# A two-layer encoder on one core: which gate products run in the seven-product scheme, and the order of the branches around the attention

## The chip, the cores and the metric

The kernel runs on one core of one Trainium2 chip. The metric is the device time of one launch in microseconds (us). TensorE (PE) multiplies matrices, VectorE (DVE) and ScalarE (ACT) work element by element, GpSimd (POOL) does little here, and SyncE (SP) issues the DMAs.

## The reference, cut to what matters

```python
for l in range(DEPTH):                              # DEPTH = 2, SEQ = D_MODEL = 1024
    h = rmsnorm(x, norm_pre[l])
    (hq, hf_f, hf_b, hi, hz, ca, cb, cz, sb, sc, sv, sz,
     aq, ak, av, az, mq, mz) = split_cols(h @ w_in[l])            # 256 columns each, ak and av 128
    y_hg = hgrn2_branch(hq, hf_f, hf_b, hi, hz, lower_bounds[l], hg_onorm[l])   # two-way scan
    y_cf = conformer_branch(ca, cb, cz, conf_dw_w[l], ...)        # 31-tap convolution, layer norm
    y_sc = short_conv_branch(sb, sc, sv, sz, sc_w[l])             # 3-tap convolution
    y_at = window_attention(aq, ak, av, ...) * jax.nn.silu(az)    # banded, blocks of 128
    mem_kv = rmsnorm(mem, mem_norm[l]) @ w_mem_kv[l]
    y_mem = memory_cross_attention(mq, mem_kv) * jax.nn.silu(mz)
    merged = None
    for n, yb in enumerate((y_hg, y_cf, y_sc, y_at, y_mem)):      # five branches
        term = jax.nn.sigmoid(h @ w_gate[l, n]) * (yb @ w_branch[l, n])
        merged = term if merged is None else merged + term
    x = x + rmsnorm(merged @ w_out[l], norm_post[l])
```

The gate `h @ w_gate[l, n]` is a product of 1024 by 1024 by 1024 for each of five branches, in float32.

## The kernel before

**Precision.** Each float32 operand is split into two parts, hi and lo (`split`: an ACT cast, then a DVE subtraction), and a product is three matmuls of 512 columns: hi by hi, lo by hi, hi by lo (`mm3`). A projection item (128 output columns, both token halves) is 48 such matmuls, and so is each of the two items of a branch output (`branch_items`).

**Order.** All engines' orders are written out by the program. `drive` takes items (`Item`: a preparation that loads and splits weights, and a body with the matmuls) from the generator `program` one after another. The next item's preparation is put out ahead of the present item's body. Between groups of three matmuls `plan.poll` puts out pieces of side work (scan, attention, convolution, norms) whose inputs should be ready by the planner's own clock. Side work with `idle="DVE"` is put out only when the planner's DVE clock is not ahead of its PE clock. An item with a `need` waits (`plan.wait`) until side work has set that flag; what this side work puts on PE stands ahead of the item's matmuls in PE's queue.

**Gates.** The five gates are 20 pairs of 128 output columns (branch n, pair g). A plain pair is two `gate_item`s of 48 matmuls. A pair in `strassen_items` uses seven products of half size, 7 x 12 = 84 matmuls; for it DVE forms sums of weights (`split_product`) and of results (`after`), and sums of the input h (`gate_forms`, put out once per layer). The second product waits for the flag `forms`. In the kernel before 15 pairs per layer go this way. The other five (branch 2, the short convolution, and pair 0 of branch 0) are plain: `sc_g` are eight plain items, `hg_g` two. Sums for pairs 1 to 3 are stored to DRAM (`mgd`) and loaded again in `after`.

**Order of a layer before.** Scan projections with the short convolution's projections between them (`hg`, `sc`), window attention projections (ak, av, aq, az for two halves g = 0, 1), the last short-convolution projection, the convolution branch's projections (cb, ca), hz, memory attention projections (mq, mz), branch output of the short convolution (`sc_b`), one plain gate, branch output of the scan, two plain gates, branch output of the window attention, five plain gates, two plain gates of the scan branch, cz (which needs the flag `cf`), branch outputs of memory and convolution, the seven-product stage, the output projection.

**Side work that matters here.** `workers` of the window attention run half g = 0 (flags `at{l}00`, `at{l}01`), then g = 1, eight blocks each; those of the memory attention run sixteen blocks. `conv` in `conformer_items` is the 31-tap convolution on DVE: per layer 60 multiply-adds over 1024 tokens, then a layer norm whose sums over channels are matmuls (`cf_mu`, `cf_var`). It begins at the flag `merge{l}`, which the first `sc_b` item sets, and ends with the flag `cf{l}`.

**Slots.** Most tensors lie in one pool of 38 slots of 128 x 1024 float32 (`slot`).

Names of tiles are those of the profile: `ps_g` plain gates, `ps_gX`, `ps_gY`, `ps_gZ` products, `ps_b` branch outputs, `ps_o` output projection, `at_*` and `m_*` window and memory attention, `cf_*` convolution branch, `h_*` scan. Nearly every row has line 112, the line of the helper `Meter` that passes each operation on.

Of the kernel before, what the change touches and what calls it, by code (L numbers as in the profile page):

```python
# [26 lines left out]
KC = D // P  # L27
# [179 lines left out]
def encoder(ctx: ExitStack, tc: tile.TileContext, a: dict, out: bass.AP):  # L207
# [398 lines left out]
    def conformer_items(l, hT, cs):  # L606
# [9 lines left out]
        us = [None, None]  # L616

        def conv():
            yield f"merge{l}"
            for j in range(2):  # L620
                yield f"cf_u{l}{j}"
                u = us[j]
                c = cs[j] = slot(f"cf_c{j}")
                mid = CONFK // 2
                dve.tensor_scalar(out=c, in0=u, scalar1=wt[:, j, mid:mid + 1], scalar2=vec[:, j, 0:1],
                                  op0=ALU.mult, op1=ALU.add)
                for k in range(CONFK):
                    if k == mid:
                        continue
                    o = k - mid  # L630
                    dst = c[:, max(0, -o):T - max(0, o)]
                    src = u[:, max(0, o):T - max(0, -o)]
                    dve.scalar_tensor_tensor(out=dst, in0=src, scalar=wt[:, j, k:k + 1], in1=dst,
                                             op0=ALU.mult, op1=ALU.add)
                    if k % 2:
                        yield
            for s in range(2):
                both = h2("cf_sum")
                dve.tensor_tensor(out=both, in0=cs[0][:, hs(s)], in1=cs[1][:, hs(s)], op=ALU.add)
                mu = yield from summed("cf_mu", mean_w, both)  # L640
                sq = []
                for j in range(2):
                    c = cs[j][:, hs(s)]
                    dve.tensor_tensor(out=c, in0=c, in1=mu, op=ALU.subtract)
                    sq.append(h2(f"cf_sq{j}"))
                    act.activation(out=sq[j], in_=c, func=AF.Square)
                dve.tensor_tensor(out=sq[0], in0=sq[0], in1=sq[1], op=ALU.add)
                var = yield from summed("cf_var", mean_w, sq[0])
                rs = h2("cf_rs")
                dve.tensor_scalar(out=rs, in0=var, scalar1=EPS, scalar2=None, op0=ALU.add)  # L650
                act.activation(out=rs, in_=rs, func=AF.Sqrt)
                dve.reciprocal(out=rs, in_=rs)
                yield
                for j in range(2):
                    c = cs[j][:, hs(s)]
                    dve.tensor_tensor(out=c, in0=c, in1=rs, op=ALU.mult)
                    th = h2("cf_t")
                    act.activation(out=th, in_=c, func=AF.Tanh, scale=half[:, j, 0:1], bias=half[:, j, 1:2])
                    dve.tensor_scalar(out=c, in0=c, scalar1=vec[:, j, 1:2], scalar2=vec[:, j, 2:3],
                                      op0=ALU.mult, op1=ALU.add)  # L660
                    dve.scalar_tensor_tensor(out=c, in0=th, scalar=1.0, in1=c, op0=ALU.add, op1=ALU.mult)
                yield
            plan.flags.add(f"cf{l}")
# [428 lines left out]
    def branch_items(l, n, ys, pbd, need=None, flag=None):  # L1092
# [4 lines left out]
        for q in range(2):  # L1097
            def prep(q=q):
                done = split_w(lambda raw: [(raw, wb[:, :, hs(q)])], [P, 2, HALF], f"b{n}{q}")

                def put():
                    if q == 0:
                        plan.wait(need)
                        for j, y in enumerate(ys):
                            yT.append((slot(f"yh{n}{j}", F32R), slot(f"yl{n}{j}", F32R)))
                            split(*yT[j], y)
                    return done()

                return put

# [101 lines left out]
    def strassen_items(l, groups, forms, pbd, mg, mgd, mT):  # L1212
# [4 lines left out]
        N = len(order)  # L1217
        raws, sums, banks, ws, late, pbs = {}, {}, {}, {}, [], {}
        state = {"loaded": 0, "split": 0}

        def load_group(gi):
            n, g = groups[gi]
# [33 lines left out]
        def merge(gi, dd, s, th):  # L1256
            n, g = groups[gi]
            m, pb = mg[g][s][:, dd, :], pbs[gi][dd]
            dve.scalar_tensor_tensor(out=th, in0=th, scalar=1.0, in1=pb[:, hs(s)], op0=ALU.add, op1=ALU.mult)
            dve.tensor_tensor(out=m, in0=m, in1=th, op=ALU.add)  # L1260

        def gate(gi, dd, s, th, src=None):
            act.activation(out=th, in_=th if src is None else src, func=AF.Tanh, scale=0.5)
# [13 lines left out]
        def after(k):  # L1277
# [3 lines left out]
            if name == "P1":  # L1281
# [3 lines left out]
                if g not in mg:  # L1285
                    mg[g] = []
                    for s in range(2):
                        mg[g].append(slot(f"mg{s}").rearrange("p (k t) -> p k t", k=2))
                        load(out=mg[g][s], in_=mgd[g][s])
                pbs.pop(gi - 1, None)  # L1290
                pbs[gi] = []
                for dd in range(2):
# [134 lines left out]
    with tc.manual_schedule(engines={mybir.EngineType.PE, mybir.EngineType.DVE, mybir.EngineType.Activation,  # L1427
# [30 lines left out]
        def program():  # L1458
# [22 lines left out]
            for l in range(NL):  # L1481
                o_hg, y_sc, y_cf, y_at, y_mem = ([None, None] for _ in range(5))
                lead, hg, hz = hgrn_items(l, hT, o_hg)
                if l == 0:
                    yield lead[0]
                    load_x(4, 5)
                    yield lead[1]
                    load_x(6, 7)
                    yield from lead[2:6] + mem_items[:2] + lead[6:7] + mem_items[2:] + lead[7:]
                else:  # L1490
                    yield from [mem_items[0], lead[0], mem_items[1], lead[1], mem_items[2], lead[2], mem_items[3]] + lead[3:]
                sc = short_conv_items(l, hT, y_sc)
                yield from hg[:1] + sc[0] + hg[1:] + sc[1][:3]
                yield from window_items(l, hT, y_at)
                yield from sc[1][3:]
                cf, cz = conformer_items(l, hT, y_cf)
                yield from cf
                mem = memory_attention_items(l, hT, kv, y_mem)
                yield from hz + mem
                mT = [[[None] * 4 for _ in range(2)] for _ in range(2)]  # L1500
                pbd = [[dram.tile([P, T], F32, name=f"pb{l}{n}{d}") for d in range(KC)] for n in range(5)]
                mgd = [[dram.tile([P, 2, HALF], F32, name=f"mg{l}{g}{s}") for s in range(2)] for g in range(4)]
                mg = {0: [None, None]}
                sc_g = [gate_item(l, 2, d, hT, pbd[2], mg[0], mgd[d // 2] if d > 1 else None, True)
                        for d in range(KC)]
                hg_g = [gate_item(l, 0, d, hT, pbd[0], mg[0], None, False) for d in range(2)]
                forms = {}
                plan.side(gate_forms(l, hT, forms))
                at_b = branch_items(l, 3, y_at, pbd[3], need=f"at{l}")
                mem_b = branch_items(l, 4, y_mem, pbd[4], need=f"mem{l}")  # L1510
                cz[1].flag = f"plain{l}"
                sc_b = branch_items(l, 2, y_sc, pbd[2])
                sc_b[0].flag = f"merge{l}"
                yield from sc_b
                yield from sc_g[:1] + branch_items(l, 0, o_hg, pbd[0]) + sc_g[1:3] + at_b + sc_g[3:] + hg_g
                yield from cz + mem_b + branch_items(l, 1, y_cf, pbd[1])
                groups = [(n, g) for g in range(4) for n in ((3, 4, 1) if g == 0 else (0, 3, 4, 1))]
                yield from strassen_items(l, groups, forms, pbd, mg, mgd, mT)
                gpost = cache(lambda l=l: row_bcast(a["norm_post"][l], f"gpost{l}"))
                x_src, hT = (x_mid if l else x_in), [None, None]  # L1520
# [43 lines left out]
```

## Time and profile before

| | us |
|---|---|
| median of 3 runs | 2317.66 (2316.72 to 2319.61) |
| the profiled execution | 2313.68 |
| its span, first to last instruction | 2311.9 |
| PE, DVE, ACT busy in the span | 2252.7, 1601.1, 971.9 |
| mean granted TensorE clock | 0.994 of full |

Busy time counts an instruction from its start to its end. Matmuls overlap in the pipeline, so a row of one shows about 0.39 us where the next begins 0.227 us later. "Idle before" is the time an engine stood still ahead of an instruction, with the instruction that ended it. Layer 1 runs from 0 to about 1172 us, layer 2 from there; the two look alike apart from their openings.

### The profile page before, as it was taken

What the parts mean: (1) busy time and instruction counts of PE and PEld (TensorE: products, weight loads), DVE (VectorE), ACT (ScalarE), POOL (GpSimd) and SP (SyncE); (2) the same over time, 40 slices, a digit from 0 to 9 for tenths busy, and PEclk for the clock granted to TensorE, in tenths of its full rate; (3) what the DMA queues carried; (4) which work ended last, traced back from release to release, by engine and by line L of the source; (5) the groups of instructions that cost most, each with busy time, mean ns of one, the idle gap of its engine ahead of it and who ended that gap; (6) DMA issues with size and microseconds to landing.
All of it is one profiled execution on the core that took longest, in us unless ns stands there. A gap on an engine that the chain in (4) does not pass through costs nothing.

```text
span 2311.9 us, 30491 instructions
## 1 busy us (share of the span) xinstructions
PE 2252.7 (97%) x11560; PEld 1843.1 (80%) x11560; DVE 1601.1 (69%) x2798; ACT 971.9 (42%) x1948; POOL 26.8 (1%) x41
## 2 busy tenths in 40 slices
PE   8899999999999999999999999999999999999998
PEld 6777788888887888887887778888878878888876
DVE  5767745446987688888667686453579787888865
ACT  5333335345434533335542433443453354333342
POOL 0000000000000000000110000000000000000000
PEclk9999999999999999999999999999999999999999
DMA  6102021103542633335440111211145525333344
GB/s 201 47 16 74 19 57 40 37 28 118 171 158 86 241 128 128 110 110 186 169 129 19 37 37 35 38 45 45 37 160 173 159 87 205 128 128 110 92 155 164
DMA packets 248019, 237.35 MB, mean 103 GB/s; under 512 B 29984, under 2 KB 191008, under 8 KB 247872
## 3 DMA queue, kind: packets, MB, share of 16 engines
q1 hardware_dynamic: 247872, 235.40, 31.4%
q8 instruction: 91, 1.49, 0.3%
q14 instruction: 56, 0.46, 0.1%
HBM read 177.69 MB, written 57.67 MB: 102 GB/s over the span
## 4 chain that ended last, share of the span: by engine, by line
PE 89%; DVE 7%; ACT 2%; issue 1%; DMA 0%; SPq 0%; POOL 0%; DVEq 0%; ACTq 0%; POOLq 0%
PE ps_gY L112 10%; PE ps_b L112 10%; PE ps_g L112 9%; PE ps_gX L112 7%; PE ps_o L112 7%; PE ps_gZ L112 7%; PE ps_hf L112 4%; PE h_s L112 3%; PE ps_hi L112 2%; PE ps_cb L112 2%; PE ps_hq L112 2%; PE ps_ca L112 2%; PE ps_sc L112 2%; PE ps_at_z L112 2%; PE ps_sz L112 2%; PE ps_hz L112 2%
## 5 line engine op out<-in xcount | busy, mean ns | idle before, releaser
L112 DVE TENSOR_TENSOR lo<-raw_g,hi 128x512 fp32r<-128x512 f32 x220 | 149.6, 687 | 95.0 <-ACT hi L112 94.7
L112 DVE SCALAR_TENSOR_TENSOR cf_c<-cf_u,cfw,cf_c 128x1009 f32<-128x1009 f32 (+14 forms) x120 | 153.0, 1275 | 3.0
L112 ACT CAST hi<-raw_g 128x512 fp32r<-128x512 f32 x220 | 133.6, 617 | 51.2 <-PE ps_gY L112 46.2
L112 PE MATMUL ps_b<-yh,lo 128*128 128x512 f32 x320 | 126.2, 394 | 7.5 <-DVE lo L112 7.5
L112 PE MATMUL ps_b<-yh,hi 128*128 128x512 f32 x320 | 128.8, 402 | 0.0
L112 PE MATMUL ps_b<-yl,hi 128*128 128x512 f32 x320 | 126.0, 394 | 0.0
L112 ACT COPY pb_out<-ps_b 128x512 f32<-128x512 f32 x160 | 91.1, 593 | 74.1 <-PE ps_b L112 57.2
L112 DVE TENSOR_TENSOR lo<-raw_in,hi 128x512 fp32r<-128x512 f32 x120 | 77.3, 686 | 46.2 <-ACT hi L112 46.0
L112 ACT ACTIVATE g_e<-g_e 128x512 f32<-128x512 f32 x60 | 38.0, 634 | 134.7 <-DVE g_e L112 134.7
L112 PE MATMUL ps_gX<-h_0h,hi 128*128 128x512 f32 x240 | 93.4, 389 | 0.0
L112 PE MATMUL ps_gX<-h_0h,lo 128*128 128x512 f32 x240 | 93.4, 389 | 0.0
L112 PE MATMUL ps_gX<-h_0l,hi 128*128 128x512 f32 x240 | 93.4, 389 | 0.0
L112 PEld LDWEIGHTS h_s<-hQQ,hkp 64*128 64x128 f32 x896 | 61.0, 192 | 25.0 <-issue 14.1
L112 ACT CAST hi<-raw_in 128x512 fp32r<-128x512 f32 x120 | 68.9, 619 | 26.4 <-PE ps_ca L112 13.1
L112 PE MATMUL h_s<-hQQ,hkp 64*128 64x128 f32 x896 | 73.7, 299 | 5.8 <-ACT hkp L112 2.9
L112 PEld LDWEIGHTS ps_b<-yh,lo 128*128 128x128 f32 x320 | 61.0, 191 | 19.8 <-DVE lo L112 8.4
L112 DVE COPY_PREDICATED hS<-masks,h_s 128x512 f32<-128x512 uint8 x112 | 75.2, 725 | 0.0
L112 DVE TENSOR_TENSOR lo<-raw_wo,hi 128x512 fp32r<-128x512 f32 x64 | 42.2, 688 | 45.6 <-PE ps_o L112 28.5
L112 PEld LDWEIGHTS ps_b<-yh,hi 128*128 128x128 f32 x320 | 60.8, 190 | 14.4 <-issue 2.7
L112 PEld LDWEIGHTS ps_b<-yl,hi 128*128 128x128 f32 x320 | 60.7, 190 | 13.1
L112 ACT COPY hkp<-hK 128x512 f32<-128x512 f32 x56 | 37.2, 664 | 80.5 <-DVE hK L112 80.5
L112 ACT ACTIVATE at_p<-at_p,at_nmx 128x384 f32<-128x384 f32 (+1 forms) x64 | 37.2, 582 | 61.6 <-DVE at_nmx L112 31.7
(555 smaller groups left out, 6486.1 us busy)
## 6 DMA issues: line engine op xcount, KB each, us to landing
raw_g<-in_w_gate_dram SPq DMA_DIRECT2D x80, 512.0 KB, 3.6
pb<-pb_out SPq DMA_DIRECT2D x160, 256.0 KB, 2.3
pb<-pb SPq DMA_DIRECT2D x80, 512.0 KB, 4.8
raw_in<-in_w_in_dram SPq DMA_DIRECT2D x68, 512.0 KB, 3.8
raw_wo<-in_w_out_dram SPq DMA_DIRECT2D x32, 512.0 KB, 5.1
raw_b<-in_w_branch_dram SPq DMA_DIRECT2D x20, 512.0 KB, 4.9
mg<-g_th SPq DMA_DIRECT2D x24, 256.0 KB, 2.2
mg<-mg SPq DMA_DIRECT2D x12, 512.0 KB, 5.3
```

Source lines behind the costliest of these rows:

```text
L112: return f(*args, **kw)
```

## The change

In words: the list of pairs in the seven-product stage grows from 15 to 18 per layer (all of branches 0, 1, 3, 4, and pairs 2 and 3 of branch 2). Four plain items of branch 2 are left. For pairs of branch 2 the first merge writes the sum (`firsts`) instead of adding to a loaded one. `conv` waits for the flag `at{l}01`, the second worker of the window attention's first half. The branch output of the short convolution moves ahead of the window attention's values and queries. The convolution branch's projections stand between the attention's two halves, hz behind the memory projections, the plain gates and the scan's branch output behind hz, then cz, then the branch outputs of window attention, convolution and memory. `gate_forms` has `idle="DVE"`. In `branch_items` the weights are split ahead of the branch's own input. In the first layer's opening the memory projections alternate with the second half's scan projections.

```diff
--- before.py
+++ after.py
@@ -616,7 +616,7 @@
         us = [None, None]
 
         def conv():
-            yield f"merge{l}"
+            yield f"at{l}01"
             for j in range(2):
                 yield f"cf_u{l}{j}"
                 u = us[j]
@@ -1099,12 +1099,13 @@
                 done = split_w(lambda raw: [(raw, wb[:, :, hs(q)])], [P, 2, HALF], f"b{n}{q}")
 
                 def put():
+                    w = done()
                     if q == 0:
                         plan.wait(need)
                         for j, y in enumerate(ys):
                             yT.append((slot(f"yh{n}{j}", F32R), slot(f"yl{n}{j}", F32R)))
                             split(*yT[j], y)
-                    return done()
+                    return w
 
                 return put
 
@@ -1217,6 +1218,7 @@
         N = len(order)
         raws, sums, banks, ws, late, pbs = {}, {}, {}, {}, [], {}
         state = {"loaded": 0, "split": 0}
+        firsts = {i for i, (n, g) in enumerate(groups) if n == 2}
 
         def load_group(gi):
             n, g = groups[gi]
@@ -1256,8 +1258,10 @@
         def merge(gi, dd, s, th):
             n, g = groups[gi]
             m, pb = mg[g][s][:, dd, :], pbs[gi][dd]
-            dve.scalar_tensor_tensor(out=th, in0=th, scalar=1.0, in1=pb[:, hs(s)], op0=ALU.add, op1=ALU.mult)
-            dve.tensor_tensor(out=m, in0=m, in1=th, op=ALU.add)
+            dst = m if gi in firsts else th
+            dve.scalar_tensor_tensor(out=dst, in0=th, scalar=1.0, in1=pb[:, hs(s)], op0=ALU.add, op1=ALU.mult)
+            if gi not in firsts:
+                dve.tensor_tensor(out=m, in0=m, in1=th, op=ALU.add)
 
         def gate(gi, dd, s, th, src=None):
             act.activation(out=th, in_=th if src is None else src, func=AF.Tanh, scale=0.5)
@@ -1286,7 +1290,8 @@
                     mg[g] = []
                     for s in range(2):
                         mg[g].append(slot(f"mg{s}").rearrange("p (k t) -> p k t", k=2))
-                        load(out=mg[g][s], in_=mgd[g][s])
+                        if gi not in firsts:
+                            load(out=mg[g][s], in_=mgd[g][s])
                 pbs.pop(gi - 1, None)
                 pbs[gi] = []
                 for dd in range(2):
@@ -1486,35 +1491,29 @@
                     load_x(4, 5)
                     yield lead[1]
                     load_x(6, 7)
-                    yield from lead[2:6] + mem_items[:2] + lead[6:7] + mem_items[2:] + lead[7:]
+                    yield from lead[2:4]
+                    for x in zip(lead[4:], mem_items):
+                        yield from x
                 else:
                     yield from [mem_items[0], lead[0], mem_items[1], lead[1], mem_items[2], lead[2], mem_items[3]] + lead[3:]
                 sc = short_conv_items(l, hT, y_sc)
-                yield from hg[:1] + sc[0] + hg[1:] + sc[1][:3]
-                yield from window_items(l, hT, y_at)
-                yield from sc[1][3:]
+                win = window_items(l, hT, y_at)
                 cf, cz = conformer_items(l, hT, y_cf)
-                yield from cf
-                mem = memory_attention_items(l, hT, kv, y_mem)
-                yield from hz + mem
+                cz[1].flag = f"plain{l}"
                 mT = [[[None] * 4 for _ in range(2)] for _ in range(2)]
                 pbd = [[dram.tile([P, T], F32, name=f"pb{l}{n}{d}") for d in range(KC)] for n in range(5)]
                 mgd = [[dram.tile([P, 2, HALF], F32, name=f"mg{l}{g}{s}") for s in range(2)] for g in range(4)]
                 mg = {0: [None, None]}
-                sc_g = [gate_item(l, 2, d, hT, pbd[2], mg[0], mgd[d // 2] if d > 1 else None, True)
-                        for d in range(KC)]
-                hg_g = [gate_item(l, 0, d, hT, pbd[0], mg[0], None, False) for d in range(2)]
+                sc_g = [gate_item(l, 2, d, hT, pbd[2], mg[0], mgd[d // 2] if d > 1 else None, True) for d in range(4)]
                 forms = {}
-                plan.side(gate_forms(l, hT, forms))
-                at_b = branch_items(l, 3, y_at, pbd[3], need=f"at{l}")
-                mem_b = branch_items(l, 4, y_mem, pbd[4], need=f"mem{l}")
-                cz[1].flag = f"plain{l}"
-                sc_b = branch_items(l, 2, y_sc, pbd[2])
-                sc_b[0].flag = f"merge{l}"
-                yield from sc_b
-                yield from sc_g[:1] + branch_items(l, 0, o_hg, pbd[0]) + sc_g[1:3] + at_b + sc_g[3:] + hg_g
-                yield from cz + mem_b + branch_items(l, 1, y_cf, pbd[1])
-                groups = [(n, g) for g in range(4) for n in ((3, 4, 1) if g == 0 else (0, 3, 4, 1))]
+                plan.side(gate_forms(l, hT, forms), idle="DVE")
+                yield from hg[:1] + sc[0] + hg[1:] + sc[1] + win[:1] + branch_items(l, 2, y_sc, pbd[2])
+                yield from win[1:4] + cf + win[4:]
+                mem = memory_attention_items(l, hT, kv, y_mem)
+                yield from mem + hz + sc_g[:1] + branch_items(l, 0, o_hg, pbd[0]) + sc_g[1:] + cz
+                yield from branch_items(l, 3, y_at, pbd[3], need=f"at{l}")
+                yield from branch_items(l, 1, y_cf, pbd[1]) + branch_items(l, 4, y_mem, pbd[4], need=f"mem{l}")
+                groups = [(n, g) for g in range(4) for n in ((0, 3, 4, 1) if g < 2 else (2, 0, 3, 4, 1))]
                 yield from strassen_items(l, groups, forms, pbd, mg, mgd, mT)
                 gpost = cache(lambda l=l: row_bcast(a["norm_post"][l], f"gpost{l}"))
                 x_src, hT = (x_mid if l else x_in), [None, None]
```

## Rows read from the trace of the kernel before

**Rows 1.** The page: busy us, share of span and instructions by engine; chain by engine.
```profile
PE 2252.7 (97%) x11560; PEld 1843.1 (80%) x11560; DVE 1601.1 (69%) x2798; ACT 971.9 (42%) x1948; POOL 26.8 (1%) x41
...
PE 89%; DVE 7%; ACT 2%; issue 1%; DMA 0%; SPq 0%; POOL 0%; DVEq 0%; ACTq 0%; POOLq 0%
```

**Rows 2.** The chain in order of time: start us, us, what.
```profile
599.38 21.76 PE ps_g L112 x96
...
791.57 2.72 PE ps_gX L112 x12
```

**Rows 3.** The longest wait of PE, 287 to 800: total us, times, longest.
```profile
PE ps_b L112 <- DVE lo L112: 3.8, 1, 3.8
```

**Rows 4.** Stretches: length, busy PE, PEld, DVE, ACT, POOL (instructions), granted clock, DMA share, GB/s.
```profile
339.80:395.30 55.50, 55.21 (x332) 45.36 (x331) 32.88 (x109) 27.93 (x75) 0.00 (x0) 1.00 0.16 46
395.30:451.80 56.50, 56.50 (x335) 45.82 (x334) 26.28 (x97) 24.90 (x69) 0.00 (x0) 1.00 0.10 29
451.80:495.30 43.50, 43.50 (x194) 36.02 (x194) 14.56 (x22) 15.51 (x32) 0.00 (x0) 1.00 0.16 49
495.30:547.50 52.20, 51.96 (x310) 41.70 (x309) 30.05 (x77) 29.82 (x76) 0.00 (x0) 1.00 0.14 49
547.50:594.00 46.50, 46.50 (x263) 36.75 (x262) 36.06 (x64) 25.18 (x59) 0.00 (x0) 1.00 0.45 149
594.00:675.30 81.30, 81.30 (x360) 67.32 (x359) 75.18 (x74) 26.09 (x45) 0.00 (x0) 1.00 0.54 179
675.30:720.70 45.40, 45.40 (x202) 37.58 (x201) 29.47 (x41) 21.30 (x32) 0.00 (x0) 1.00 0.47 145
720.70:742.50 21.80, 21.80 (x98) 18.02 (x96) 19.63 (x30) 10.10 (x17) 0.00 (x0) 1.00 0.01 1
742.50:791.50 49.00, 45.23 (x194) 36.94 (x193) 36.96 (x55) 29.90 (x54) 0.00 (x0) 0.97 0.61 214
791.50:1077.10 285.60, 285.60 (x1262) 236.49 (x1261) 229.44 (x355) 113.31 (x198) 0.00 (x0) 1.00 0.39 131
```

**Rows 5.** Groups of DVE, 791.5 to 1077.1: busy, mean ns, idle before.
```profile
L112 DVE TENSOR_TENSOR lo<-raw_g,hi 128x512 fp32r<-128x512 f32 x88 | 60.5, 688 | 45.1 <-ACT hi L112 45.1
...
L112 DVE TENSOR_TENSOR raw_g<-raw_g 128x512 f32<-128x512 f32 x15 | 10.4, 692 | 0.5
```

**Rows 6.** One of three stretches of 10 us, columns as in Rows 4.
```profile
320.00:330.00 10.00, 10.00 (x46) 8.24 (x45) 1.82 (x4) 1.75 (x3) 0.00 (x0) 1.00 0.29 53
```

**Rows 7.** DVE groups, 547.4 to 675.3; the convolution's ends on the timelines.
```profile
L112 DVE SCALAR_TENSOR_TENSOR cf_c<-cf_u,cfw,cf_c 128x1009 f32<-128x1009 f32 (+14 forms) x60 | 76.5, 1275 | 1.5
...
547.45 0.81 DVE L112 TENSOR_SCALAR cf_c<-cf_u,cfw,cfv 128x1024 f32<-128x1024 f32 x1
675.30 0.69 DVE L112 TENSOR_TENSOR cf_sum<-cf_c,cf_c 128x512 f32<-128x512 f32 x1
717.77 0.39 PE L112 MATMUL cf_var<-cf_varl,mean_w 128*128 128x512 f32 x1
720.71 0.39 PE L112 MATMUL ps_cz<-h_0h,hi 128*128 128x512 f32 x1
```

**Rows 8.** Timeline: first and last step of the attention's first half.
```profile
343.06 0.28 PE L112 MATMUL at_s<-at_k0a,at_q 128*128 128x256 f32 x1
394.88 0.29 DVE L112 SCALAR_TENSOR_TENSOR at_z<-at_o,at_z 128x128 f32<-128x128 f32 x1 [3.01 <-PE at_o L112]
```

**Rows 9.** PE ahead of the memory branch's output; busy time by 2 us.
```profile
746.63 0.79 PE L112 MATMUL ps_b<-yh,lo 128*128 128x512 f32 x1 [3.77 <-DVE lo L112]
...
746.00:748.00 2.00, 1.37 (x3) 1.16 (x4) 1.97 (x4) 0.00 (x0) 0.00 (x0) 0.51 0.00 0
748.00:750.00 2.00, 2.00 (x7) 1.53 (x6) 1.93 (x4) 0.83 (x2) 0.00 (x0) 0.64 0.00 0
```

**Rows 10.** The two longest waits of PE in the opening, 60 to 120.
```profile
PE h_s L112 <- ACT mT L112: 2.6, 1, 2.6
PE ps_mkv L112 <- DVE lo L112: 2.4, 1, 2.4
```

## The prediction

> **What bounds the kernel now.** I read the busy table and the chain of waits first, then the middle of a layer in stretches, then the places where TensorE (PE) waits. PE is busy 97% of the span, VectorE (DVE) 69%, and PE holds 89% of the chain that ended last [rows 1]. The busy figure alone could hide slack inside the matmuls, so I looked at the spacing: in the seven-product stage one product of 12 matmuls follows the last every 2.72 us, and 96 matmuls of a plain gate pair take 21.76 us [rows 2]. Both are 0.2267 us a matmul, so this is PE at its pace, with nothing between. From 287 to 800 us the one PE wait over half a microsecond is 3.8 us [rows 3], and in the seven-product stage never (285.60 of 285.60 us busy [rows 4]). Work removed from PE's stream therefore comes off the time, as long as what feeds PE keeps up. The feeder is DVE. Its load is uneven: 15 to 33 us of busy time in the stretches up to 547.5, then 75.18 of 81.3 us while the 31-tap convolution runs, then 229.44 of 285.60 us in the seven-product stage [rows 4]. The question is what the new order does to DVE in the middle of a layer.
>
> **The change, part by part (per layer; there are two layers alike).**
>
> 1. *Three more gate pairs as seven products.* Twelve matmuls fewer per pair: 12 x 0.2267 = 2.72 us [rows 2], three pairs, two layers: **-16.3 us** on PE. Per pair DVE gains 12 operations (3 splits, 4 sums of weights, 5 of results) of about 0.69 us [rows 5], 8.2 us. They fall in the seven-product stage, where a pair now costs DVE 229.44/15 = 15.3 us against 84 x 0.2267 = 19.0 us of PE. The two short-convolution pairs there add less still, because their first merge writes the sum and needs no addition. PE keeps the pace at 80% DVE load, ScalarE (ACT) is at 113.31 of 285.60 [rows 4]: cost nothing. Without that cover the 12 operations would cost 8.2 us a pair.
>
> 2. *Fewer merges through DRAM.* Eight stores of 256 KB and four loads of 512 KB a layer disappear from SP's queue. DMA is at 0.39 in that stage [rows 4], and nothing on PE waits for it: nothing either way.
>
> 3. *The branch output of the short convolution moves ahead of the attention.* The same 21.76 us of PE work, between the keys' and the values' projection. DVE was nearly idle there, 1.82 us busy in 10 [rows 6], so its splits, eight times 512 columns at 0.69 [rows 5], are hidden; without that cover they would be 5.5 us. It starts the first attention half 33 us later: 21.8 us for this block and 10.9 for the last short-convolution projection, which now stands ahead too.
>
> 4. *The convolution starts after the first attention half instead of after the first branch item, and has less PE work to hide behind.* This is the term that decides. Before, the convolution's first tap ran at 547.45, the first sum after its last tap at 675.30, and the last variance matmul, which the "cz" projections stand behind on PE, at 717.77; cz began at 720.71, 3 us later [rows 7]. DVE carried 36.06 + 75.18 + 29.47 = 140.7 us in those 173.2 us [rows 4], 81%.
> After the change I build the same stretch from rows. The first half of the attention runs from 343.06 to 394.88 [rows 8], 52 us; starting 33 us later it ends near 428. PE then has to cz: six us of the last "ca"; twelve items of 48 matmuls (two of attention, four of memory, two hz, four plain gates), 10.88 us each, and one branch output of 96, 21.76 [rows 2]; and small attention matmuls. Those I take by difference: seven items (76.2 us) took 339.8 to 451.8 with sixteen attention blocks, so eight blocks cost 17.9 us; and 76.2 us of items took 495.3 to 599.4 [rows 2, 4] with the memory attention, 27.9 us. Together 6 + 152.3 + 45.8 = **204 us of cover**.
> DVE's load in it: 26.28 us of 395.3 to 451.8 less 2.1 for "ca"; 14.56 + 30.05 less 5.8 for the moved branch block and a first tap; 36.06 less 19.1 of taps; and eighteen splits, copies and gate steps of 0.69 that these stretches don't hold, 12.4; in all 92. The convolution itself: 60 taps of 1.275 and two of 0.81, 78 us [rows 7]; its norm up to the last variance, 17. Together **187 us, 92% of 204**. DVE reached 92.5% of 594.0 to 675.3, with no attention running, but 77.5% of 547.5 to 594.0, with the memory attention [rows 4]. At the first rate 187 us take 202 us: no stall. At the second for the 160 us with attention, then the first, 227 us: 23 us late in each layer. So the bounds are 0 and 23 us of PE wait at cz per layer. I take 5, nearer the lower end: two attentions and the taps give DVE more to choose from than the one that ran at 77.5%.
> A PE wait also costs clock. After the 3.77 us gap at 742.9 the granted clock was 0.51 and 0.64 in the next two stretches of 2 us [rows 9], against 1.00 in the stretch before [rows 4]: 1.2 GHz in place of 2.4 for most of them. Ten matmuls began there, three and seven, where fifteen fit between the gap's end and 750.0; five lost are 1.1 us. The cz wait is thus **+2 x (5 + 1.1) = +12.2 us**.
> The Trainium skill (TensorE: Matmul & The Clock Gate, "HAM oscillation") says the same of gaps: an array that has idled is throttled again and has to work itself free. The trace agrees.
>
> 5. *The sums of the normed input ("forms") only in DVE's idle time, and weights split before the branch's own input.* Before, these sums stood ahead of the splits of the memory branch, and PE waited 3.77 us for a "lo" [rows 3, 9], with 1.1 us of clock behind. Now they give way, and PE has cz and three branch blocks, 87 us, ahead of the products, for 19.63 + 36.96 and 5.2 more for the attention's branch, 62 us of DVE [rows 4]. I take both waits as gone: **-2 x 4.9 = -9.7 us**; the other bound is 0.
>
> 6. *The opening.* The first memory projection moves ahead of one half-projection (24 matmuls, 5.4 us), yet it waits for the normed memory. PE waited in six places between 60 and 120 us, 2.6 us the longest; one, 2.4, was for a late "lo" of the memory weights [rows 10]. Bounds: -2.4 (that wait goes) to +5.4 (the half-projection no longer fills the first). I take **+2**. Layer 2 opens as before.
>
> 7. hz behind the memory projections, the attention's branch behind cz: the same PE work, and their inputs are ready long before. Nothing.
>
> **Sum.** The profiled execution took 2313.7 us (span 2311.9 and 1.8 around it): 2313.7 - 16.3 + 12.2 - 9.7 + 2.0 = 2301.9. The median of the runs shown lies 4.0 above that execution, so the median I predict is **2306 us**, 0.5% less.
>
> **Rivals.**
> *The convolution is late (slower).* In parts 1 and 5 the gain is 26.0 us, less 2 for the opening. If cz waits S us per layer, the cost is 2 x (S + 1.1), so it breaks even at S = 10.9, which is DVE at 187/215 = 87% through the stretch. For it: 77.5% with one attention running, 81% over the whole of the stretch before, and the norm's chain at the end, 42.5 us from 675.30 to 717.77 with DVE two thirds busy. Against it: 92.5% where taps filled. At S = 17 it gives 2313.7 - 16.3 - 9.7 + 36.2 + 2.0 + 4.0 = **2330**. A second road leads to the same place: the kernel has 38 slots, and second attention half, taps and memory attention together want some 39 to 41 by my count from the code, so copies may wait for a slot. The Trainium skill (Perfetto Trace Analysis, "Optimization Strategy") reads repeated gaps on the engine that should be full as a sign of too few buffers; no run here shows it for this order.
> *The wait eats the gain (no change).* S between 8.6 and 13: about **2318**.
> *The change does only half of what it says.* If the memory branch's wait stays (the sums still stand in front) and S is 5: 2306 + 9.7 = **2316**, within the same bound.
> *DVE paces the seven products.* It would have to take 24% more per pair (19.0 against 15.3 us) than the rows show; 2 in 100, counted with the slower case.
>
> **How the numbers follow.** 0.2% is 4.6 us, about what a measurement of this kernel can tell from no change. Forecast (S up to 8.6): 57 in 100. No change, from the second and third: 17. Late convolution and the rest: 26. The low end is S = 0 with the opening's better bound, 2313.7 - 16.3 - 9.7 - 2.4 + 4.0 = 2289; the high end S = 17 with the opening's worse bound, 2333. I give 2290 to 2333; beyond the upper end lie some 12 in 100, and a few below the lower.
>
> **What would show it.** Right: 1512 matmuls a layer in the seven-product stage, 12 every 2.72 us, some 343 us long; no wait for a "lo" at the memory branch; the last cf_var matmul within 5 us of the end of the last plain gate; DVE over 88% busy between the first tap and there. Wrong: a PE gap of over 10 us ahead of ps_cz with cf_var named as what ends it, and a granted clock of half behind it; or waits for "lo" all through the memory projections, with DVE full; or an opening longer by more than 6 us.

## The result and the profile after

| | before | after |
|---|---|---|
| median, us | 2318.64 (2316.72 to 2320.82) | 2336.82 (2335.37 to 2339.07) |
| the profiled execution's span, us | 2311.9 | 2333.6 |
| mean granted TensorE clock | 0.994 | 0.987 |

The median before counts one run more than the table ahead of the change. The ratio is 1.0079, interval 1.0062 to 1.0096: 18 us slower. The prediction said 2306 and 2290 to 2333; the time lies above the range, on the side of the first rival.

The page, busy times and chain by engine, against [rows 1]: PE's busy time fell by 4.8 us, yet the span grew by 21.7, and VectorE and ScalarE together hold 12% of the chain in place of 9.

```profile
PE 2247.9 (96%) x11488; PEld 1837.7 (79%) x11488; DVE 1644.3 (70%) x2870; ACT 996.4 (43%) x1982; POOL 27.3 (1%) x41
...
PE 85%; DVE 8%; ACT 4%; issue 2%; DMA 0%; SPq 0%; POOL 0%; DVEq 0%; ACTq 0%; POOLq 0%
```

What PE waited for from 430 to 760 us (total, times, longest), against [rows 3], where one wait of 3.8 us was the only one over half a microsecond:

```profile
PE cf_mu L112 <- ACT cf_muh L112: 4.9, 1, 4.9
PE cf_var L112 <- ACT cf_varh L112: 3.4, 1, 3.4
PE at_t L112 <- ACT m_p L112: 3.1, 1, 3.1
PE at_t L112 <- DVE at_p L112: 2.0, 2, 1.7
PE at_o L112 <- ACT at_pT L112: 1.6, 1, 1.6
PE ps_b L112 <- ACT pb_out L112: 1.3, 1, 1.3
PE ps_b L112 <- DVE th_cz L112: 1.1, 1, 1.1
PE at_s L112 <- ACT m_p L112: 1.0, 1, 1.0
```

Two groups: 8.3 us for the norm of the convolution ahead of cz, and some 7.7 us inside the two attentions. The wait for a "lo" is gone. The stretches of layer 1 (columns as in [rows 4]), from the first tap to the last, from there to the last cf_var, the wait ahead of cz, cz, the three branch outputs, the products:

```profile
417.70:614.00 196.30, 188.59 (x1051) 154.14 (x1050) 162.20 (x307) 88.46 (x224) 0.00 (x0) 0.99 0.19 61
614.00:650.90 36.90, 28.54 (x118) 22.35 (x117) 22.46 (x31) 16.84 (x25) 0.00 (x0) 0.91 0.28 93
639.50:650.70 11.20, 2.84 (x5) 1.36 (x5) 7.01 (x11) 5.72 (x9) 0.00 (x0) 0.70 0.48 165
650.70:674.30 23.60, 23.60 (x98) 19.35 (x97) 19.22 (x27) 10.23 (x15) 0.00 (x0) 0.93 0.00 1
674.30:744.30 70.00, 66.83 (x290) 53.61 (x289) 42.11 (x61) 42.65 (x76) 0.00 (x0) 1.00 0.63 225
744.30:1087.00 342.70, 342.70 (x1514) 283.76 (x1513) 271.13 (x419) 135.29 (x237) 0.00 (x0) 1.00 0.37 122
```

The product stage is full: 342.7 of 342.7 us busy, at the clock of 1.00, with VectorE at 79%. While taps run, VectorE is at 162.20/196.30 = 83%. In the 36.9 us behind the last tap it is at 22.46/36.90 = 61% and ScalarE at 46%: nobody is full there, and PE waits. The chain of work in time (start, us, what; pieces of under 0.6 us left out) shows why:

```profile
643.14 0.61 DVE cf_sum L112
643.78 0.63 ACT cf_muh L112
644.45 1.53 PE cf_mu L112 x2
646.61 0.69 DVE cf_c L112
647.33 0.64 ACT cf_sq L112
647.99 0.70 DVE cf_sq L112
648.71 0.63 ACT cf_varh L112
649.38 1.53 PE cf_var L112 x2
```

Sum, cast, matmul, subtraction, square, sum, cast, matmul: each step on another engine waits for the one before. And this is the second token half; the first went through the same steps from 614.0 to 642, and the code of `conv` starts the second only when the first is done. PE's granted clock meanwhile, in rows of 2 us (busy PE, clock, DMA share, GB/s):

```profile
641.00:643.00 2.00, 0.00 (x0) 1.00 0.10 40
643.00:645.00 2.00, 0.55 (x1) 0.74 0.87 254
645.00:647.00 2.00, 0.97 (x2) 0.50 0.99 348
...
651.00:653.00 2.00, 2.00 (x6) 0.50 0.00 0
653.00:655.00 2.00, 2.00 (x8) 0.70 0.04 8
655.00:657.00 2.00, 2.00 (x11) 1.00 0.00 0
```

PE stood from 639.5 to 644.4; the clock fell to 1.2 GHz from 2.4 at 643.9, while it stood, and rose again at 654.2, 3.5 us into cz.

### The profile page after: what moved, and what is told of

The parts are those of the page before. It is cut to its first block, busy times and chain, and to the rows that moved or that the text cites. A ratio compares the mean times of both kernels' runs of the same rounds, so it can differ in the third digit from the quotient of the medians.

```text
span 2333.6 us, 30426 instructions
## 1 busy us (share of the span) xinstructions
PE 2247.9 (96%) x11488; PEld 1837.7 (79%) x11488; DVE 1644.3 (70%) x2870; ACT 996.4 (43%) x1982; POOL 27.3 (1%) x41
## 4 chain that ended last, share of the span: by engine, by line
PE 85%; DVE 8%; ACT 4%; issue 2%; DMA 0%; SPq 0%; POOL 0%; DVEq 0%; ACTq 0%; POOLq 0%
PE ps_gY L112 12%; PE ps_gX L112 8%; PE ps_b L112 8%; PE ps_gZ L112 8%; PE ps_o L112 7%; PE ps_hf L112 4%; PE ps_g L112 3%; PE h_s L112 3%; PE ps_cb L112 2%; PE ps_ca L112 2%; PE ps_hz L112 2%; PE ps_sc L112 2%; PE ps_sz L112 2%; PE ps_aq L112 2%; PE ps_at_z L112 2%
## 5 line engine op out<-in xcount | busy, mean ns | idle before, releaser
L112 DVE TENSOR_TENSOR lo<-raw_g,hi 128x512 fp32r<-128x512 f32 x232 | 159.0, 688 | 116.7 <-ACT hi L112 116.7
L112 ACT CAST hi<-raw_g 128x512 fp32r<-128x512 f32 x232 | 141.9, 616 | 60.5 <-PE ps_gY L112 56.2
L112 ACT ACTIVATE g_e<-g_e 128x512 f32<-128x512 f32 x72 | 45.6, 634 | 161.3 <-DVE g_e L112 161.3
L112 PE MATMUL ps_gX<-h_0h,hi 128*128 128x512 f32 x288 | 112.1, 389 | 0.0
L112 PE MATMUL ps_gX<-h_0h,lo 128*128 128x512 f32 x288 | 112.1, 389 | 0.0
L112 PE MATMUL ps_gX<-h_0l,hi 128*128 128x512 f32 x288 | 112.0, 389 | 0.0
L112 ACT CAST hi<-raw_wo 128x512 fp32r<-128x512 f32 x64 | 37.8, 621 | 60.9 <-PE ps_o L112 47.0
```

The source lines that it names most:

```text
L112: return f(*args, **kw)
```

## The experiments

Two theories came from these rows. **Theory 1:** the convolution is late, and cz's wait is what went wrong. **Theory 2:** apart from that, the new order costs some 9 us a layer where the second half of the window attention and the memory attention now run together. Ratios are to the kernel before on the same chip; the kernel before had medians of 2318.8 to 2319.4 us there. Each edit is made to the changed kernel unless it says otherwise.

### e1_order15: the new order with the old fifteen pairs

```diff
-sc_g = [gate_item(l, 2, d, ...) for d in range(4)]
+sc_g = [gate_item(l, 2, d, ...) for d in range(KC)]
+hg_g = [gate_item(l, 0, d, ...) for d in range(2)]
-... + sc_g[1:] + cz
+... + sc_g[1:] + hg_g + cz
-groups = [(n, g) for g in range(4) for n in ((0, 3, 4, 1) if g < 2 else (2, 0, 3, 4, 1))]
+groups = [(n, g) for g in range(4) for n in ((3, 4, 1) if g == 0 else (0, 3, 4, 1))]
```

> The new order with the old fifteen pairs: ten plain gates instead of four stand ahead of cz, 65.3 us more TensorE work to hide the convolution behind; the product stage has 57.1 us less. Theory 1, the cz wait is all that went wrong (8.4 us idle and 1.8 us of clock per layer, 20.4 us in all): it vanishes, nothing else is lost, and the time is that of the kernel before less the 9.7 us foreseen for the memory branch, 2309 to 2319 us. Theory 2, the new order also loses some 9 us per layer between the second window half and the memory attention (7.7 us idle and 1.7 of clock in layer 1), whatever the products are: the cz wait vanishes, the waits for at_p, at_pT and m_p of 1.6 to 3.1 us stay, and the time is 2330 to 2338 us, about that of the changed kernel, because the cz wait happens to cost what three pairs save.

Measured: 2323.26 us, ratio 1.0014 (1.0004 to 1.0024); span 2319.6. Waits of PE from 430 to 800 us:

```profile
PE at_t L112 <- ACT m_p L112: 3.1, 1, 3.1
PE at_t L112 <- DVE at_p L112: 2.0, 2, 1.7
PE at_o L112 <- ACT at_pT L112: 1.6, 1, 1.6
PE ps_b L112 <- ACT pb_out L112: 1.5, 2, 1.2
PE at_s L112 <- ACT m_p L112: 1.0, 1, 1.0
```

The waits for cf_mu and cf_var are gone and those in the attentions are all there, to the tenth. The time lies between the two forecasts. Mine for theory 2 left out that the new order also saves what the wait for "lo" cost. In the rows theory 2 holds: the order alone has these waits, whatever the pairs, and costs 0.14% with them.

This run also separates the terms, because it differs from the changed kernel only in pairs and cover. From the first matmul of ak to the first product (both read off PE's timeline):

```profile
305.10:744.20 439.10, 419.85 (x2138) 341.64 (x2138) 291.47 (x547) 208.25 (x452) 0.00 (x0) 0.98 0.28 94
```
```profile
305.30:795.00 489.70, 480.48 (x2425) 394.08 (x2424) 309.70 (x575) 221.99 (x476) 0.00 (x0) 1.00 0.31 102
```

The first is the changed kernel, the second e1, which has six plain gates more in it, 65.3 us by the rate of [rows 2]. 489.7 - 65.3 = 424.4, so the late convolution costs the changed kernel 439.1 - 424.4 = **14.7 us** a layer: 11.2 of standing and slow norm matmuls (which in e1 took 0.9 among the gates), 1.7 in cz (23.6 against 21.9), 2.4 in the branch outputs behind (70.0 against 67.6).

### e2_at_ahead and e7_at_ahead_mem: more cover

```diff
-... + sc_g[1:] + cz
-yield from branch_items(l, 3, y_at, pbd[3], need=f"at{l}")
+... + sc_g[1:] + branch_items(l, 3, y_at, pbd[3], need=f"at{l}") + cz
```

In e2 the convolution's branch output stands right behind cz, and since the next item's input is split ahead of the present item's matmuls, it is computed from what cz hadn't written yet. In e7 the memory's branch output stands between the two, which mends that.

> The changed kernel with the branch output of the window attention ahead of cz, where it stands after cz now: 21.8 us more cover, eighteen pairs. Theory 1: the wait for cf_mu and cf_var goes, 2336.8 - 20.4 = 2316 us, with the last cf_var done by the end of that branch output. Rival: VectorE gets the splits of that branch (5.5 us) ahead of the last steps of the norm and the convolution only ends later, so that part of the wait stays: 2325 to 2333 us. Theory 2 adds that the waits at at_t and at_o stay at 7.7 us per layer.

> The window attention's branch output ahead of cz, as in the second run, and the memory's branch output between cz and the convolution's, so that the convolution's branch reads what cz has written. The order of work up to cz is that of the second run, so all theories expect its time, 2308.8 us within 4, and no wait for cf_mu or cf_var.

Measured: 2308.79 us, 0.9955 (0.9940 to 0.9970), and 2309.59 us, 0.9958 (0.9941 to 0.9974). In both no wait for cf_mu or cf_var is left, and the attentions' waits stay. 21.8 us of cover that were already in the program, put one place further ahead, turn 0.8% slower into 0.4% faster. From ak to the first product e2 took 424.0 us (305.1 to 729.1), what was worked out above for a convolution that is not late. The rival was right that the convolution ends later, but not on the cost: the last cf_var came 6 us later than in the changed kernel (656.2 against 650.1), but still within the moved branch output (639.2 to 662.0).

### e6_norms_apart: the chain itself

```diff
-            for s in range(2):
-                both = h2("cf_sum")
 ...
+            for s in range(2):
+                plan.side(norm(s))
+            for s in range(2):
+                yield f"cf_n{l}{s}"
```

> The changed kernel with the layer norm of the convolution's two token halves as two pieces of side work that run beside each other, where one followed the other (614.0 to 650.9 us, with VectorE 60% busy). Theory 1 in the form of a chain, the convolution is late because the norm's steps follow one another from engine to engine and not because VectorE is full: the time from the first cf_sum to the last cf_var falls from 36.9 to about 22 us, the cz wait of 15.1 us per layer goes, 2336.8 - 2 x (13 to 15) = 2307 to 2311 us. Rival, VectorE's throughput is the limit, as the working of the prediction has it: the last cf_var comes within 5 us of where it is now, 2326 to 2338 us.

Measured: 2319.68 us, 1.0008 (0.9999 to 1.0017). From the last tap to the last cf_var:

```profile
612.80:629.30 16.50, 16.50 (x75) 13.66 (x73) 10.82 (x17) 8.24 (x13) 0.00 (x0) 1.00 0.10 34
```

The taps take 196.3 us, as in the changed kernel to the tenth, and the norm up to the last cf_var 16.5 instead of 36.9. cz began at 639.0, right behind the gates, with no cover added. The operations are the same in number, but not up to that point: VectorE did 10.82 us of work there where it did 22.46, because the first half's steps behind its own cf_var (the reciprocal among them, 7.2 to 7.9 us) and some gate steps now come later. `norm(s)` also goes out without the `idle="DVE"` of `conv`, so the run doesn't separate the two halves' order from the planner's rule. It does show that the same taps, at the same pace, leave time enough for cz once the second half needn't stand behind the whole of the first. The time is some 10 us above the forecast. Counted from ak, cz began 10.5 us earlier than in the changed kernel; but the norms' last steps now fall among the splits of the branch outputs, which took 73.6 us (661.0 to 734.6) where e1 took 67.6, and so some 6 of the 14.7 us are lost again.

### e9_conv_at_scan: an earlier start

```diff
-            yield f"at{l}01"
+            yield f"scan{l}"
```

> The changed kernel with the convolution free to start as soon as its own input is there (it waits for the scan's flag, long set, in place of the window attention's first half): its first input was complete at 407.8 us, its first tap ran at 417.7. Theory 1, cz is late by a fixed chain behind the taps: everything up to the last cf_var moves up by 8 to 10 us and the cz wait of 15.1 us per layer falls to 3 to 6: 2336.8 - 2 x (9 to 12) = 2313 to 2319 us. Rival: the early taps hold up the window attention's first half on VectorE, what follows starts later by as much, and the last cf_var stays where it is: 2332 to 2342 us.

Measured: 2321.76 us, 1.0016 (1.0007 to 1.0026). The first tap moved to 414.2 only, the last to 606.5, the last cf_var to 644.0, 37.5 us behind. cz began at 644.2, 1.1 us behind the last plain gate. The time is some 3 us above the forecast. The wait went from both ends: the last cf_var came 6.9 us earlier, and the last plain gate ended 3.6 us later (643.1 against 639.5), as the rival said of what follows. More cover, the halves side by side and an earlier start each remove the wait.

### e11_no_mem_blocks: the memory attention's blocks left out

```diff
-            for b in range(par, NT, 2):
...
             plan.flags.add(f"mem{l}{j}{par}")
```

> The changed kernel without the sixteen blocks of the memory attention (the stacking of its keys and its projections stay; its branch carries the projection alone, so the output lacks the attention over the memory). Theory 2 in the form of two attentions sharing four small PSUM banks and ScalarE: the waits at 511 and 524 us of 3.11 and 0.97 us, which m_p ends, go; those at 471 and 476 us of 1.70 and 1.64 us stay, as the sixteen casts stay; the cz wait goes as well, since VectorE loses its steps, and the time falls by 2 x (15.1 + 4 + 1.7) and the blocks' own matmuls, to some 2240 to 2270 us. Rival, the window attention's second half waits by itself: a wait for at_p or m_p's successor of about 3 us stays near 511 us.

Measured, in one run: 2273.53 us, just above the forecast. Waits of PE from 430 to 780 us:

```profile
PE cf_mu L112 <- ACT cf_muh L112: 5.6, 1, 5.6
PE cf_var L112 <- ACT cf_varh L112: 3.4, 1, 3.4
PE at_o L112 <- ACT at_pT L112: 2.1, 2, 1.6
PE at_t L112 <- DVE at_p L112: 2.0, 2, 1.7
```

The waits ended by m_p, 3.1 and 1.0 us, are gone: without the overlap of the two attentions they don't arise. Those ended by at_p and at_pT stay. And cz waits as long as ever, where I had expected no wait: the blocks' own matmuls were cover too. The last tap moved up by 28 us (585.9), the last plain gate's end by 31 (608.8), and the chain behind the last tap took 34.6 us. Less load on VectorE alone didn't help.

### e3_hz_first and e4_both: the attentions pulled apart

```diff
-yield from mem + hz + sc_g[:1] + ...
+yield from hz + mem + sc_g[:1] + ...
```

e4 has the move of e2 as well, and its convolution's branch output reads too early as there.

> The changed kernel with hz ahead of the memory projections, so that 21.8 us of TensorE work stand between the window attention's last projection and the memory attention's first. Theory 2, two attentions at once share ScalarE, four small PSUM banks and slots: the waits for at_p, at_pT and m_p of 1 to 3 us go (9 us per layer), VectorE's share in this stretch rises from 56 to 89% towards 90%, and the cz wait shrinks too: 2336.8 - 18 = 2319 us or less. Rival: the waits only move, since the memory attention now starts 21.8 us later, on top of the convolution's taps, and the cz wait grows by as much: 2332 to 2342 us.

> Both moves: hz ahead of the memory projections and the window attention's branch output ahead of cz. If theories 1 and 2 both hold and their costs are separate, 2336.8 - 20.4 - 18 = 2298 us, faster than the kernel before by 0.8%. If the two waits are one loss seen in two places (VectorE's slow rate in the first is what makes the convolution late in the second), the sum is less: about 2316 us, as either move alone.

Measured: 2370.21 us, 1.0220 (1.0205 to 1.0235), and 2338.93 us, 1.0085 (1.0070 to 1.0100). Of e3, 430 to 780 us:

```profile
PE cf_mu L112 <- ACT cf_muh L112: 18.4, 2, 13.2
PE cf_var L112 <- ACT cf_varh L112: 6.9, 2, 3.5
PE at_t L112 <- DVE at_p L112: 1.8, 2, 1.6
PE ps_b L112 <- DVE yl L112: 1.4, 2, 1.2
PE at_o L112 <- ACT at_pT L112: 1.0, 1, 1.0
```

The rival was right, and by more than it said. The m_p waits went, 4.1 us; but the memory attention's steps now fell among the taps. The last tap came at 640.7 instead of 614.0 while the cover still ended at 636.9, so both halves' chains stood in the open, 25 us of waits. This shows the norm alone, with no gate's step beside it (columns as in [rows 4]):

```profile
640.70:667.90 27.20, 5.73 (x8) 2.45 (x9) 15.83 (x20) 9.73 (x13) 0.00 (x0) 0.50 0.14 53
```

It takes 27 us though VectorE is free for nearly half of them. e4's move gave the same chain 21.8 us of cover and took 31 us off, but the last cf_var still came 16 us behind the moved branch output (657.9 to 674.3), so neither sum held. The other attention waits stayed, so "two attentions at once" is only part of theory 2.

### e5_keys_early, e12_keys_aside and e8_three: the key casts

ScalarE's work in the changed kernel as the window attention's second half starts, and VectorE's longest wait from 454 to 486 us:

```profile
462.83 6.63 ACT L112 CAST m_k<-mK 64x256 fp32r<-64x256 f32 x16
469.49 0.58 ACT L112 CAST m_q<-ps_mq 64x512 fp32r<-64x512 f32 x1
```
```profile
DVE m_q L112 <- ACT m_q L112: 9.9, 3, 8.6
```

Sixteen casts stand in a row, then the one that VectorE waits for, and behind VectorE's waiting subtraction the attention's steps that PE waits for. The Trainium skill (PSUM — Partial Sum Buffer, "Engine vs sequencer instructions") says that ScalarE's and VectorE's queues are strictly first in, first out; these rows agree. e5 puts the row out between the convolution branch's projections, e12 (on e7) as side work of single casts that goes out only when the planner has ScalarE free (the attention's blocks wait for a flag that it sets):

```diff
-                if s == 0 and j == 0:
-                    stack_keys()
 ...
+        plan.side(stack_keys(), idle="ACT")
```

e8 is e5, e6 and e7 together.

> The changed kernel with ScalarE's sixteen casts that stack the memory's keys (m_k, 6.5 us in one row at 462.8 to 469.5 us, ahead of the casts of m_q and the window attention's at_pT) put out between the convolution branch's projections, where ScalarE is a third busy. If these casts are what crowds the two attentions: VectorE's 8.6 us wait for m_q goes, the TensorE waits of 1.70 and 1.64 us behind it go (3.6 us per layer with the small one), the taps end some 7 us earlier and the cz wait (15.1 us per layer with its clock, as the new order with fifteen pairs showed by its absence) shrinks by as much: 2336.8 - 2 x (3.6 + 7) = 2316 us, down to 2305 if the later waits of 3.1 and 1.0 us go as well. Rival, two attentions at once are too many for four small banks whatever ScalarE does: the waits at at_t stay, taps end at the same time, 2332 to 2338 us.

> The order of run e7 with the sixteen key casts as side work that goes out two steps apart, one cast at a time, only when ScalarE is free by the planner's clock, from the window attention's last two projections on. If the row of sixteen casts is the cause of the waits of 1.70 and 1.64 us and of VectorE's 8.6 us wait for m_q, and if moving them to the first half only put them ahead of other work that was due (as in e5, where the first tap came 4 us later and the last 11 us later), then these waits go and nothing comes later: 2309.6 - 2 x (3.6 to 6) = 2298 to 2303 us. Rival: each cast is due work of ScalarE wherever it stands, and the waits only change their names: 2306 to 2313 us.

> The three together: keys stacked early, norms side by side, the window attention's branch output ahead of cz and the memory's between cz and the convolution's. If the attention's waits come from the sixteen casts, 2308.8 - 2 x (3.6 to 9) = 2291 to 2302 us, 0.8 to 1.2% faster than the kernel before; the norms side by side add nothing here, since the cz wait is gone already. If the casts are not the cause, 2305 to 2312 us, as with the branch output alone.

Measured: e5 2345.86 us, 1.0115 (1.0100 to 1.0131); e12 **2302.34 us, 0.9929 (0.9914 to 0.9944)**; e8 2329.76 us, 1.0044 (1.0030 to 1.0059). e12 came out as forecast, e5 and e8 above both of their forecasts. The longest wait of PE in e12, 430 to 780 us:

```profile
PE at_t L112 <- ACT at_pT L112: 2.6, 2, 2.1
```

VectorE's longest wait for m_q is 1.9 us in place of 8.6. The waits of 1.7, 1.6 and 3.1 us are gone, one of 2.1 us has come: the attentions' waits are 4.0 us in layer 1 where e7 has 7.7, and 7 us are won on e7 by the medians, 5 between the profiled executions. e12 is the fastest kernel of this study, 0.7% ahead of the kernel before. In e5 the attentions' waits went in the same way, but the casts ran at 376 to 383 us, inside the first attention half; the first tap came 4 us later and the last 11 us later (625.3), and cz paid: 12.8 and 3.4 us of waits. Why 4 us became 11 I can't say. e8 removed that wait and met another, for ScalarE's copies of the moved branch output (638 to 680 us, where the norms' steps now lie too; the branch output took 36.9 us instead of e7's 22.8):

```profile
PE ps_b L112 <- ACT pb_out L112: 7.3, 3, 4.1
```

### e10_old_order18: the pairs alone

```diff
 # the kernel before, with the new list of pairs and merges
-sc_g = [gate_item(l, 2, d, ...) for d in range(KC)]
-hg_g = [gate_item(l, 0, d, ...) for d in range(2)]
+sc_g = [gate_item(l, 2, d, ...) for d in range(4)]
 ...
```

> The old order with eighteen pairs: six plain gates, 65.3 us of TensorE work, leave the stretch ahead of cz, and nothing else is moved. Theory 1: the convolution's taps and norm end about where they did less the removed gates' VectorE steps (six items of some 4 us), 25 us earlier, so cz waits 65 - 25 = 40 us per layer, and the time is 2318.6 - 16.3 + 80 = 2382 us (2360 to 2400). Rival, the matmuls saved are what counts and VectorE catches up when the gates are gone: 2302 to 2320 us.

Measured: 2394.53 us, 1.0330 (1.0313 to 1.0348). Waits of PE, 430 to 780 us:

```profile
PE cf_mu L112 <- ACT cf_muh L112: 31.6, 2, 18.4
PE cf_var L112 <- ACT cf_varh L112: 6.9, 2, 3.5
PE ps_b L112 <- DVE lo L112: 5.6, 1, 5.6
```

Theory 1's number within 13 us. The norm ran alone here too, 26.8 us from the first cf_sum at 673.4 to the last cf_var. The plain gates are what the convolution hides behind; take them away and nothing else, and the saving of 16 us turns into a loss of 75. The new order gives 58 of them back.

## Why the prediction was wrong

The terms, both layers, against the spans (2311.9 to 2333.6):

| term | predicted | measured | from |
|---|---|---|---|
| three more pairs | -16.3 | -16.4 | stage 342.7 against 285.6 [rows 4], 57.1 more; six gates, 65.3, less |
| cz's wait | +12.2 | +29.4 | 2 x 14.7, e1 against the changed kernel |
| rest of the order | -9.7 | +7.6 | ak to products: before 496.8; e1 489.7, and 10.9 for the projection that now stands ahead of ak; 2 x (500.6 - 496.8) |
| the opening | +2 | -0.5 | first ak at 305.1; before 294.7, plus 10.9 |
| sum | -11.8 | +20.1 | span +21.7 |

Some 1.6 us more are in layer 2's output projection, whose matmuls took 91.1 us where those of the kernel before took 89.5.

**Part 1 was right**: 12 matmuls every 2.72 us, 1512 a layer, VectorE at 79%.

**Part 4 is the step that failed.** It took VectorE at 92.5% throughout, and in its 187 us of work the norm stood as 17 us, so that taps and norm would take 202 us. The load came out well, 184.66 us; the rate didn't. The stretch took 233.2 us, 31 more. The rows it drew on showed the norm as a chain of 42.5 us [rows 7]; the text names that figure only for the rival. With 42.5 in place of 18 the same working gives 184 + 42.5 - 204 = 22 us late, the upper bound, and the forecast would have been the rival's. The two pieces came out so:

| VectorE, us | expected | measured |
|---|---|---|
| first tap to last, work / length | 170 / 184 (170/0.925) | 162.2 / 196.3 |
| last tap to last cf_var, work / length | 17 / 18 | 22.46 / 36.9 |

In length 19 of the 31 us are the norm. Of its 36.9 us some 15.2 are VectorE's own steps for it, 7.3 are splits and gate steps that fell in between, and in 14.4 VectorE stood, where the forecast had left 1.4. Where nothing else was there to do, it still took 27 us with 15.83 of work (e3; e10 the same), some 4 of which are norm matmuls at the lower clock. With more work in between it took longer: 42.5 us in the kernel before, with 27.7 of VectorE work. So the norm goes by the length of its chain and by what stands between its steps.

The rest is the rate while taps ran, 83%: VectorE stood for 34 us there, where the forecast had left 14. What holds it at 83% stays open; the taps go out under `idle="DVE"`, by the planner's own clock, and no run was made without that.

The cover was longer than built, 221.8 us (417.7 to 639.5) against 204. It ended 7.5 us later than the 632, about what the attentions' waits come to, and began 10 us earlier, because the first attention half took 42.5 us (374.8 to 417.3) where 52 were taken over from the kernel before. So two errors, 31 us in the stretch and 18 in the cover, partly cancel. With the cover as built cz would have waited near 29 us by this sum; that it was 11 is luck.

The waits named cf_mu and cf_var as that rival said, ended by the casts behind which they stood; VectorE was at 79% from the first tap to there (184.66 of 233.2 us), not over 88.

The clock behind the gap was priced at 1.1 us; it was 1.7 in cz alone, since the gap was longer and its slow norm matmuls lay in it.

**Parts 5 and 7: a gain that came, and a cost I didn't look for.** The wait for "lo" at the memory branch is gone, as forecast. But hz behind the memory projections was priced at nothing, and it is what puts the memory attention's blocks beside the window attention's second half: with hz first (e3) the m_p waits are gone. Both attentions and the key casts share ScalarE's queue and four small PSUM banks; e11 shows 4.1 us a layer of waits that go with the overlap, and e12, which keeps the overlap and spreads the casts, wins 7 us on e7. The 3.1 us wait went in both, so it needed the overlap and the row of casts together.

**The opening** was 2.5 us better than taken; its bounds held.

The rival "convolution late" had the right place. Its price for the wait, 36.2 us, is 7 above the 29.4 measured; what took the time past its 2330 is the attentions. What the rival's second road says of 38 slots wasn't tried; no wait shown here is put down to a slot.

## What to carry to other kernels

Price a chain that goes from engine to engine by its length in time, as the trace shows it, and not by its busy time over a rate: behind the last of a long row of operations, the chain is what the next engine waits for. That length has a floor, which shows where the chain runs alone (27 us here), and grows with the other work that stands between its steps (to 42.5 us). When work is removed from the engine that bounds, list what was hidden behind it; here the same pairs cost 75 us where the cover went with them (e10) and gained some 14 where another cover was put in its place (e7 against e1). And when two pieces of side work are made to run together, go through each in-order queue that both use for a row of operations of one that the other will stand behind.

## What the runs showed of the hardware

The clock: a stand of 4.9 us followed by two lone matmuls and another of 3.4 left TensorE at 1.2 GHz for 10 us, 643.9 to 654.2, so that two stands of 8.3 us together cost 14.7, what came late behind them included. And a reciprocal of 128x512 took VectorE 3.35 us where its other operations of that size in the norm took 0.55 to 0.69. It comes once for each half; the first half's stood in the middle of the chain, ahead of the second half's sum:

```profile
L112 DVE RECIPROCAL cf_rs<-cf_rs 128x512 f32<-128x512 f32 x1 | 3.4, 3352 | 2.0 <-ACT cf_rs L112 2.0
```
